# A two-layer diffusion backbone on one core: modulation sums six pieces deep, mixer transfers on one queue, inverses placed by stream step

## The chip, the core and the metric

The kernel runs on one core of one Trainium2 chip. The core has TensorE (PE, matmuls; PEld is its weight loads), VectorE (DVE), ScalarE (ACT), GpSimd (POOL), and SyncE (SP), which only issues transfers. ACT and POOL can issue transfers too. Every engine works through its own instructions in the order in which the program holds them, and waits on semaphores for the others. The metric is the device time of one execution in microseconds (us).

## The reference, cut to what matters

Two layers over 256 latent tokens (and, in the first layer, 256 context tokens), width 2048, all in float32:

```
for l in (0, 1):
    sh1, sc1, g1, sh2, sc2, g2 = split(silu(c) @ ada_w[l] + ada_b[l], 6)     # ada_w[l]: 2048 x 12288
    h = rmsnorm(x) * (1 + sc1) + sh1
    if l == 0:   # even mixer, context hc modulated in the same way from c_ctx
        ka, va, kb, vb, a, b, qa, qb, za = split(h @ ev_w_in)        # 2048 x 7200; context: the first six
        ka, va, qa = silu(conv5(ka, va, qa)); k, q = rope(l2norm(..))
        y_gdn = gated delta rule, chunks of 64, both directions, 8 heads, started from the context's state
                (needs T = inverse of (I + lower part of beta k k^T decay) of every chunk)
        y_na  = neighbourhood attention of 8 heads over grid and context
        y = concat(norm(y_gdn) * silu(za), y_na) @ ev_w_out
    else:        # odd mixer: short gated convolution
        y = (b * conv3(c_ * v)) @ od_w_out
    x = x + g1 * y
    x = x + g2 * (silu(m @ w_gate) * (m @ w_up)) @ w_down            # m = rmsnorm(x) * (1 + sc2) + sh2
out = rmsnorm(x) * final_norm
```

## The kernel before

**Weight streams.** Every large product reads its weights once from HBM. `load_w` fetches 512 KB pieces (`raw`, four buffers in the mixer) on SP's queue; `split_w` makes a rounded half `whi` on ACT and the rest `wlo` on DVE; PE multiplies high by high, low by high and high by low, so that three matmuls stand for one. `fm_stream` makes outputs by feature (weights held, 256 tokens of latent and, where needed, of context streamed), `tm_stream` by token. One step of a stream is one 128-row slice of the contraction.

**Start.** The first layer's sh1 and sc1 come from PE: `start_block(b)` loads 4 MB of `ada_w` in four pieces (`araw0`, four buffers) and multiplies them by the two conditioning vectors (L477); `start_tokens(b)` turns the sums into shift and scale (L488) and modulates two slices of the tokens (transposes of `xn`, then `h_hi`, `h_lo`). The loop runs over b = 0..7, and between two blocks two steps of the first key stream `s0` (512 columns) are put.

**Mixer.** In the order of the code: the second key stream, the gates, `chunk_matrices(1)` (context: Gram matrices, decay, a 31-step substitution on DVE over 32x32 blocks, with a turn through HBM to regroup the blocks: `dl`, `lsol`, `dz`), `inverses` for both head groups (blocks joined to 128x128 on PE, from pieces `xd`, `xdT`, `n32`, `n64` read back from HBM), `chunk_matrices(0)`, the QA and VA streams, the scan over the context, inverses, scores and scan of the latents (`latent_scores`, `latent_quad`), the QB, KB and VB streams (their outputs are staged to HBM through two `nst` buffers, `stage`), attention head by head (`na_scores`, `na_values`; the position bias `br` is read in a strided pattern), the ZA stream, and the output product `ev_w_out`.

**Modulation sums.** The other segments of `ada_w` are summed on DVE: `ada_job` takes one piece `araw` after another (in the mixer 256 KB each, 192 in all, `AB` = 3 buffers), multiplies it by a column of c and adds it to `acc` (L332); PE sums over partitions after 16 pieces (L338). A `Pump` releases R_QB, R_KB, R_ZA or R_WO of them for each step of a stream.

**Order.** The kernel is built with a scheduler that sets each engine's order from its own estimate of durations; the code's order gives priorities. So instructions of stages that lie apart in the code stand mixed in the engines' orders, and `tc.issue_after` only says what an instruction must not be put ahead of. Transfers were issued by SP, and by ACT for stores of results (`kd`, `vd_`, `qTd`, `nd64`, `nd32`, `kb_d`, `vb_d`, `qb_d`, `zd`), half of `lsol` and `dz`, and `br`.

Of the kernel before, what the change touches and what calls it, by code (L numbers as in the profile page):

```python
# [29 lines left out]
D = 2048  # L30
# [12 lines left out]
AB = 3  # L43
R_QB = 1.2
R_KB = 1.8
R_ZA = 1.8
# [59 lines left out]
def body(tc, x, c, ctx, c_ctx, ada_w, ada_b, norm_mix, norm_ffn, ffn_w_gate, ffn_w_up, ffn_w_down,  # L106
# [122 lines left out]

    def split_w(raw, behind=None):  # L230

        hi = wp["pool"].tile([128, 1024], F32R, name="whi", tag="whi", bufs=wp["split"])
        lo = wp["pool"].tile([128, 1024], F32R, name="wlo", tag="wlo", bufs=wp["split"])
        with Stack() as order:
            for ins in behind or ():
                order.enter_context(tc.issue_after(ins.ins))
            acopy(hi, raw)
            DVE.tensor_tensor(lo, raw, hi, op=OP.subtract)  # L238
        return hi, lo

    def w_steps(segs, ks, behind=None):
# [3 lines left out]
        for g in range(0, len(ks), nk):  # L245
            assert ks[g + nk - 1] == ks[g] + nk - 1
            hi, lo = split_w(load_w(segs, ks[g], nk), behind if g // nk in (2, 3) else None)
            for j in range(nk):
                yield ks[g] + j, hi[:, j * W:(j + 1) * W], lo[:, j * W:(j + 1) * W]

# [16 lines left out]
    def tm_stream(segs, ks, lhs, toks, evac, normed=None):  # L267
# [6 lines left out]
        for i, group in grouped(((k, (hi, lo) + lhs(k)) for k, hi, lo in w_steps(segs, ks, normed)), len(ks), head):  # L274
            last = i == len(ks) - 1
            if not last:
                for ti, t in enumerate(toks if group else ()):
                    for g, (hi, lo, lh, ll) in enumerate(group):
# [7 lines left out]
                        for n in range(nb):  # L286
                            PE.matmul(ps[ti][n], b, hi[:, n * 512:(n + 1) * 512], start=False, stop=False)  # L287
# [11 lines left out]
    def fm_stream(segs, ks, ws, evac):  # L299

        ps = [None] * 4
        for i, group in grouped(((k, (k, hi, lo)) for k, hi, lo in w_steps(segs, ks)), len(ks)):
            for f in range(4):
                if i == 0:
                    ps[f] = mmt()
                for g, (k, hi, lo) in enumerate(group):
# [3 lines left out]
                    for j, (wt, mv) in enumerate(((a, h_hi), (a, h_lo), (b, h_hi))):  # L310
                        for n, w in enumerate(ws):
                            if j or i:
                                PE.matmul(ps[f][:, n * 256:(n + 1) * 256], wt, mv(w, k), start=False,  # L313
                                          stop=i == len(ks) - 1 and g == len(group) - 1 and j == 2 and w == ws[-1])
# [5 lines left out]
    def ada_job(pool_, l, seg, kind, gamma=None, width=1024, bufs=2):  # L320

        wr = ada_w[l].rearrange("(k p) n -> p k n", p=128)
        nf = width // 128
        for blk in range(D // width):
            c0 = seg * D + blk * width
            acc = pool_.tile([128, width], F32, name="acc", tag="acc", bufs=1)
            POOL.memset(acc, 0.0)
            SP.dma_start(acc[0:1, :], ada_b[l:l + 1, c0:c0 + width])
            for k in range(KT):
                raw = pool_.tile([128, width], F32, name="araw", tag="araw", bufs=bufs)  # L330
                SP.dma_start(raw, wr[:, k, c0:c0 + width])
                DVE.scalar_tensor_tensor(acc, raw, cT[:, k:k + 1], acc, op0=OP.mult, op1=OP.add)  # L332
                yield
            fs_ = slice(blk * nf, (blk + 1) * nf)
            p = smt()
            if width < 1024:
                for f in range(nf):
                    PE.matmul(p[:, f:f + 1], acc[:, f * 128:(f + 1) * 128], ones[:, 0:1], start=True, stop=True)  # L338
                pc = p
            else:  # L340
                ah = pool_.tile([128, width], F32R, name="ah", tag="ah", bufs=1)
                al = pool_.tile([128, width], F32R, name="al", tag="al", bufs=1)
                split(ah, al, acc, DVE)
                for f in range(nf):
                    for a in (ah, al):
                        PE.matmul(p[0:nf, 0:128], pick[:, nf - 1 - f:2 * nf - 1 - f], a[:, f * 128:(f + 1) * 128],
                                  start=f == 0 and a is ah, stop=f == nf - 1 and a is al)
                g = pool_.tile([16, 128], F32, name="grow", tag="grow", bufs=1)[0:nf]
                acopy(g, p[0:nf, 0:128])
                if kind == "row":  # L350
                    ACT.dma_start(row_d[l, seg][fs_], g)
                    continue
                pc = smt()
                transpose(pc[:, 0:nf], g)
            if kind == "sc":
                DVE.scalar_tensor_tensor(scc[l, seg - 1][:, fs_], pc[:, 0:nf], 1.0, gamma[:, fs_], op0=OP.add, op1=OP.mult)
            else:
                DVE.tensor_copy((shc if kind == "sh" else gcol)[l, seg][:, fs_], pc[:, 0:nf])
        if kind == "row" and width < 1024:
            p = smt()  # L360
            transpose(p[0:16, 0:128], gcol[l, seg])
            g = pool_.tile([16, 128], F32, name="grow", tag="grow", bufs=1)
            DVE.tensor_copy(g, p[0:16, 0:128])
            SP.dma_start(row_d[l, seg], g)
# [39 lines left out]
    def drive(stream, pump=None, n=1):  # L404
        for _ in stream:
            if later:
# [61 lines left out]
    def start_block(b):  # L468

        pr = gdt()  # L470
# [10 lines left out]
    def start_tokens(b, pr):  # L481
        mrow = sp.tile([128, 512], F32, name="mrow", tag="mrow", bufs=2)
        DVE.tensor_copy(mrow, pr)
        p = smt()
# [9 lines left out]
        DVE.tensor_tensor(sc0[:, kk, :], sc0[:, kk, :], g_mix[0][:, kk, None].to_broadcast([128, 2, 2]), op=OP.mult)  # L494
        for k in range(2 * b, 2 * b + 2):
# [3 lines left out]
            for w in range(2):  # L499
# [3 lines left out]
                DVE.tensor_tensor(h_lo(w, k), m, h_hi(w, k), op=OP.subtract)  # L503

# [56 lines left out]
    def head_evac(n, q, c0, done, sums):  # L561
# [3 lines left out]
        def f(i_, p):  # L565
            st_[i_] = kvp.tile([128, 512], F32, name="hst", tag="hst", bufs=4)[:, 0:n * 128]
# [3 lines left out]
            out_t = kvp.tile([128, 4, 4, 128], F32, name="hq", tag="hq", bufs=2)  # L570
# [53 lines left out]
    def ka_evac(q):  # L624
        def done(kt, ss):
            normalise(kt, 4, rstd(kvp, ss, [128, 4, 4], 16, 1.0, "rk"))
            ACT.dma_start(hslice(kd, 0, 4, q), kt.rearrange("p t h e -> p t (h e)"))
        return head_evac(4, q, 0, done, True)

    def va_evac(q):  # L630
        def done(vt, ss):
            ACT.dma_start(hslice(vd_, 0, 4, q), vt.rearrange("p t h e -> p t (h e)"))
        return head_evac(4, q, 8, done, False)

    def qa_evac(q):
        def done(qt, ss):
# [3 lines left out]
            for g in range(2):  # L640
# [6 lines left out]
                ACT.dma_start(qTd[:, q * 4 + g * 2:q * 4 + g * 2 + 2, :], qf)  # L647
# [756 lines left out]
```

## Time and profile before

| what | us |
|---|---|
| median of 3 runs (2838.1, 2841.96, 2846.2) | 2841.96 |
| the profiled execution | 2848.17 |
| its span, first to last instruction | 2846.4 |
| PE busy | 2732.5 |
| DVE busy | 1924.8 |
| ACT busy | 1308.3 |
| mean granted TensorE clock | 0.986 |

The profiled execution is 6.2 us above the median of the others, within what they spread. A busy PE is not PE at its peak: matmuls overlap, and a matmul that is issued late still counts as busy up to its modelled end. So the idle time of a stretch and the granted clock (PEclk, 1.00 is full speed) say more than the share of busy time. In the rows of waits an engine's line and tile come first, then who ended the wait, then the sum, how often, and the longest.

### The profile page before, as it was taken

What the parts mean: (1) busy time and instruction counts of PE and PEld (TensorE: products, weight loads), DVE (VectorE), ACT (ScalarE), POOL (GpSimd) and SP (SyncE); (2) the same over time, 40 slices, a digit from 0 to 9 for tenths busy, and PEclk for the clock granted to TensorE, in tenths of its full rate; (3) what the DMA queues carried; (4) which work ended last, traced back from release to release, by engine and by line L of the source; (5) the groups of instructions that cost most, each with busy time, mean ns of one, the idle gap of its engine ahead of it and who ended that gap; (6) DMA issues with size and microseconds to landing.
All of it is one profiled execution on the core that took longest, in us unless ns stands there. A gap on an engine that the chain in (4) does not pass through costs nothing.

```text
span 2846.4 us, 40363 instructions
## 1 busy us (share of the span) xinstructions
PE 2732.5 (96%) x15113; PEld 2281.6 (80%) x15113; DVE 1924.8 (68%) x2647; ACT 1308.3 (46%) x1945; POOL 51.1 (2%) x77
## 2 busy tenths in 40 slices
PE   5999999989989999999999999999999999999998
PEld 3699989888767778888888878878878888888886
DVE  3387767857667878776677768897678644445665
ACT  3267543222354544444445545444454444444554
POOL 0000001000000000000000000000000000000000
PEclk9999999999999999999999999999999999999999
DMA  9955568777758599987788657998559766656653
GB/s 345 311 177 164 143 208 253 243 225 236 210 170 278 200 318 346 347 285 249 272 305 282 198 175 243 328 319 306 179 179 332 262 188 180 195 186 215 192 192 126
DMA packets 284927, 680.78 MB, mean 239 GB/s; under 512 B 57273, under 2 KB 97313, under 8 KB 283323
## 3 DMA queue, kind: packets, MB, share of 16 engines
q1 hardware_dynamic: 262148, 652.48, 69.4%
q10 hardware_dynamic: 22583, 25.73, 3.0%
q8 instruction: 118, 1.93, 0.3%
q14 instruction: 78, 0.64, 0.1%
HBM read 657.63 MB, written 20.48 MB: 238 GB/s over the span
## 4 chain that ended last, share of the span: by engine, by line
PE 70%; DMA 15%; DVE 9%; issue 3%; ACT 2%; SPq 1%; POOL 0%; ACTq 0%; DVEq 0%; POOLq 0%
PE mm L287 17%; PE mm L285 17%; PE mm L284 17%; DMA araw<-in_ada_w_dram 11%; PE mm L313 7%; DVE acc L332 3%; DVE wlo L238 3%; PE sm L188 2%; PE mm L293 2%; PE mm L295 2%; PE mm L294 2%; DMA raw<-in_od_w_in_dram 1%; DMA acc<-in_ada_b_dram 1%; PE gd L477 1%; ACT whi L169 0%
## 5 line engine op out<-in xcount | busy, mean ns | idle before, releaser
L238 DVE TENSOR_TENSOR wlo<-raw,whi 128x1024 fp32r<-128x1024 f32 x800 | 971.5, 1222 | 452.3 <-ACT whi L169 446.3
L169 ACT ACTIVATE whi<-raw 128x1024 fp32r<-128x1024 f32 x800 | 841.9, 1058 | 875.5 <-PE mm L287 632.4
L332 DVE SCALAR_TENSOR_TENSOR acc<-araw,cT,acc 128x1024 f32<-128x1024 f32 (+1 forms) x416 | 431.2, 1037 | 228.4 <-DMA araw<-in_ada_w_dram 198.8
L285 PE MATMUL mm<-wlo,fhi 128*128 128x512 f32 x1232 | 473.6, 394 | 0.2 <-DVE wlo L238 0.2
L284 PE MATMUL mm<-whi,fhi 128*128 128x512 f32 x1232 | 470.9, 396 | 0.6 <-ACT fhi L1187 0.6
L287 PE MATMUL mm<-whi,flo 128*128 128x512 f32 x1232 | 392.2, 392 | 0.1
L284 PEld LDWEIGHTS mm<-whi,fhi 128*128 128x128 f32 x1232 | 232.4, 189 | 50.4 <-ACT fhi L1187 1.0
L287 PEld LDWEIGHTS mm<-whi,flo 128*128 128x128 f32 x1232 | 231.0, 188 | 50.7 <-DVE flo L1189 0.3
L285 PEld LDWEIGHTS mm<-wlo,fhi 128*128 128x128 f32 x1232 | 232.5, 189 | 48.7 <-DVE wlo L238 0.7
L284 PE MATMUL mm<-whi,ahi 128*128 128x512 f32 x672 | 259.8, 392 | 0.0
L285 PE MATMUL mm<-wlo,ahi 128*128 128x512 f32 x672 | 259.4, 391 | 0.0
L287 PE MATMUL mm<-whi,alo 128*128 128x512 f32 x672 | 209.7, 392 | 0.0
L313 PE MATMUL mm<-hllo,whi 128*128 128x256 f32 x640 | 181.1, 287 | 0.0
L313 PE MATMUL mm<-hlhi,wlo 128*128 128x256 f32 x600 | 169.4, 288 | 2.0 <-issue 1.5
L313 PE MATMUL mm<-hlhi,whi 128*128 128x256 f32 x600 | 167.5, 290 | 1.0 <-DVE hlhi L502 1.0
L172 ACT ACTIVATE ahi<-prodT 128x256 fp32r<-128x256 f32 x176 | 73.0, 417 | 194.7 <-PE mm L285 187.6
L285 PEld LDWEIGHTS mm<-wlo,ahi 128*128 128x128 f32 x672 | 126.2, 188 | 27.5
L284 PEld LDWEIGHTS mm<-whi,ahi 128*128 128x128 f32 x672 | 126.2, 188 | 27.2
L287 PEld LDWEIGHTS mm<-whi,alo 128*128 128x128 f32 x672 | 126.1, 188 | 27.3
L285 PE MATMUL mm<-wlo,dhi 128*128 128x512 f32 x336 | 127.3, 398 | 2.6 <-DVE wlo L238 2.4
L313 PEld LDWEIGHTS mm<-hllo,whi 128*128 128x128 f32 x640 | 124.0, 194 | 0.4
L284 PE MATMUL mm<-whi,dhi 128*128 128x512 f32 x336 | 123.5, 396 | 0.3 <-DVE u_t L1329 0.3
(399 smaller groups left out, 4055.9 us busy)
## 6 DMA issues: line engine op xcount, KB each, us to landing
araw<-in_ada_w_dram SPq DMA_DIRECT2D x288, 512.0 KB
raw<-in_ffn_w_down_dram SPq DMA_DIRECT2D x176, 512.0 KB
raw<-in_ffn_w_gate_dram SPq DMA_DIRECT2D x160, 512.0 KB
raw<-in_ffn_w_up_dram SPq DMA_DIRECT2D x160, 512.0 KB
raw<-in_ev_w_in_dram SPq DMA_DIRECT2D x112, 512.0 KB
araw<-in_ada_w_dram SPq DMA_DIRECT2D x192, 256.0 KB
raw<-in_od_w_in_dram SPq DMA_DIRECT2D x96, 512.0 KB
raw<-in_ev_w_out_dram SPq DMA_DIRECT2D x32, 512.0 KB
```

The source lines that it names most:

```text
L169: ACT.activation(dst, src, AF.Copy)
L172: ACT.activation(hi, src, AF.Copy)
L188: return PE.transpose(dst, src, ident[:n, :n])
L238: DVE.tensor_tensor(lo, raw, hi, op=OP.subtract)
L284: PE.matmul(ps[ti][n], a, hi[:, n * 512:(n + 1) * 512], start=first, stop=False)
L285: PE.matmul(ps[ti][n], a, lo[:, n * 512:(n + 1) * 512], start=False, stop=False)
L287: PE.matmul(ps[ti][n], b, hi[:, n * 512:(n + 1) * 512], start=False, stop=False)
L293: PE.matmul(ps[ti][n], lh(t), hi[:, c_], start=False, stop=False)
L294: PE.matmul(ps[ti][n], lh(t), lo[:, c_], start=False, stop=False)
L295: PE.matmul(ps[ti][n], ll(t), hi[:, c_], start=False, stop=hi is group[-1][0])
L313: PE.matmul(ps[f][:, n * 256:(n + 1) * 256], wt, mv(w, k), start=False, stop=i == len(ks) - 1 and g == len(group) - 1 and j == 2 and w == ...
L332: DVE.scalar_tensor_tensor(acc, raw, cT[:, k:k + 1], acc, op0=OP.mult, op1=OP.add)
```

## The change

- **Sums.** `ada_job` keeps only its 1024-wide form; the mixer's sums become `ada_mixer`: six pieces are loaded ahead (`AHEAD` = `AB` = 6), `acc` has two buffers, each sum is ordered behind the last `wlo` (`issue_after(last_lo)`), and the closing matmuls come three sums late (`LAG`). R_QB goes from 1.2 to 0.6, R_ZA from 1.8 to 1.5.
- **Queue.** All the mixer transfers that ACT issued are issued by SP.
- **Inverses.** The read-back is split off (`load_offdiag`, `load_diag`) and stands ahead of the QB stream; the inverses run from `plan` at counted stream steps 30, 32, 79 and 80, and their first matmuls are ordered behind the stream's last (`last_mm`). `chunk_matrices(0)` and the context's scan move behind step 32, scores and scan of the latents behind step 80.
- **Half of the second key group early.** A stream `s1` over 256 of its 512 columns runs in turn with `s0` in the start, from block 1 on; it uses the two `gd` PSUM banks, and the start's sums move to the `sm` banks. The other 256 columns follow as a stream of their own, in which deferred work is released at every second step.
- **Buffers.** `hst` has six buffers instead of four; the heads' outputs share the two `xdT` buffers.

```diff
-R_QB = 1.2
+P_INV = (30, 32, 79, 80)
+AHEAD = 6
+LAG = 3
+R_QB = 0.6
-AB = 3
+AB = 6
-R_ZA = 1.8
+R_ZA = 1.5
...
+    def ada_mixer(pool_, parts):
...
+            raws[i] = pool_.tile([128, 512], F32, name="araw", tag="araw", bufs=AB)
+            SP.dma_start(raws[i], wr[:, k, c0:c0 + 512])
+
+        def total(i):
+            n, k = divmod(i, KT)
+            with tc.issue_after(last_lo[0]):
+                DVE.scalar_tensor_tensor(accs[n], raws.pop(i), cT[:, k:k + 1], accs[n], op0=OP.mult, op1=OP.add)
...
+        for i in range(AHEAD):
+            load(i)
+        N = len(blocks) * KT
+        for i in range(N + LAG):
+            if i < N:
+                total(i)
+                load(i + AHEAD)
+            if i >= KT + LAG - 1 and (i - LAG + 1) % KT == 0:
+                close((i - LAG + 1) // KT - 1)
+            yield
...
+    def drive(stream, pump=None, n=1, every=1, counts=False):
+        for i, _ in enumerate(stream):
+            steps[0] += counts
+            while counts and plan and plan[0][0] <= steps[0]:
+                plan.pop(0)[1]()
+            if later and i % every == every - 1:
...
-        pr = gdt()
+        pr = smt()
...
-    s0 = fm_stream([(wv, C_KA, 512)], ks, [0, 1], ka_evac(0))
+    s0 = fm_stream([(wv, C_KA, 512)], ks, [0, 1], ka[0])
+    s1 = fm_stream([(wv, C_KA + 512, 256)], ks, [0, 1], ka[1], gdt)
...
+    both = in_turn(s0, s1)
     for b in range(8):
-        start_tokens(b, sums)
+        start_tokens(b, sums, both if b else iter(()))
         if b < 7:
-            next(s0), next(s0)
             sums = start_block(b + 1)
...
-    drive(fm_stream([(wv, C_KA + 512, 512)], ks, [0, 1], ka_evac(1)))
+    drive(fm_stream([(wv, C_KA + 768, 256)], ks, [0, 1], lambda f, p: ka[1](f + 2, p)), every=2)
...
-        ACT.dma_start(nd64, n64)
-        ACT.dma_start(nd32, n32)
+        SP.dma_start(nd64, n64)
+        SP.dma_start(nd32, n32)
...
-                (SP, ACT)[d].dma_start(lsol[p0:p0 + 16], dl[b, :, d * 16:(d + 1) * 16, :].rearrange("r n c -> n r c"))
+                SP.dma_start(lsol[p0:p0 + 16], dl[b, :, d * 16:(d + 1) * 16, :].rearrange("r n c -> n r c"))
...
     parts = chunk_matrices(1)
-    xdTs = [inverses(parts, q) for q in range(2)]
-    parts = chunk_matrices(0)
...
+    def second_inverse():
+        nonlocal parts, off, diag
+        xdTs.append(inverses(off, diag[1], 1))
+        parts = chunk_matrices(0)
+        for q in range(2):
+            scan(q, 1, xdTs[q])
+        xdTs.clear()
+        off = load_offdiag(parts)
+        diag = [load_diag(parts[2], q) for q in range(2)]
+
+    def latents():
+        xdTs.append(inverses(off, diag[1], 1))
+        ATs = [latent_scores(q) for q in range(2)]
+        o_ts.extend(latent_quad(q, xdTs[q], ATs[q]) for q in range(2))
...
+    plan += [(P_INV[0], first_inverse), (P_INV[1], second_inverse), (P_INV[2], first_inverse), (P_INV[3], latents)]
...
-            ACT.dma_start(br[half * 64:half * 64 + 64], src)
+            SP.dma_start(br[half * 64:half * 64 + 64], src)
```

How the built orders differ at three places follows. L188, L284, L285, L287, L313, L332, L338, L477, L488, L918, L927, L938 and L960 of before are L191, L291, L292, L294, L321, L389, L396, L533, L546, L1000, L1009, L1020 and L1042 now.

PE, in the last block of the start, before: sums of `ada_w` (`gd<-araw`), shift and scale (`mrow`), token transposes (`xn`), then stream `s0`.

```order
L477 MATMUL gd<-araw_1016,cT_120 32x512 x4
L477 MATMUL gd<-araw_1023,cT_120 32x512 x4
L477 MATMUL gd<-araw_1030,cT_120 32x512 x4
L488 MATMUL sm<-cs,mrow 128x2 x4
L188 MATMUL sm<-cs,xn 128x128 x8
L313 MATMUL mm<-hlhi,whi 128x256 x4
```

The same place now (`mm` is `s0`, `gd` is `s1`):

```order
L321 MATMUL mm<-hclo,whi 128x256
L321 MATMUL mm<-hlhi,wlo 128x256
L321 MATMUL mm<-hchi,wlo 128x256
L321 MATMUL gd<-hlhi,whi 128x256
L321 MATMUL gd<-hchi,whi 128x256
L321 MATMUL gd<-hllo,whi 128x256
L533 MATMUL sm<-araw_1138,cT_120 32x512 x4
L321 MATMUL gd<-hclo,whi 128x256
L321 MATMUL gd<-hlhi,wlo 128x256
L321 MATMUL gd<-hchi,wlo 128x256
```

Matmuls of both key streams now stand between the sums. Ahead of the last L488 there were 332 of the streams' matmuls, and ahead of the last L546 there are 479; on SP 12 `raw` pieces stood ahead of the last piece of the start's `ada_w`, and now 14.

SP, where the latents' inverse pieces are read back around the end of the first VB stream, before (the last two of eight such reads `xd`, `xdT` from `dz`; `kT`, `vtok` for the context's scan; `araw` for the sums; `raw` a stream's weights):

```order
L864 DMA xd<-dz 32x16x32
L864 DMA xdT<-dz 32x16x32
L781 DMA kT<-kTd 128x1024
L776 DMA vtok<-vd__139 128x2x512
L331 DMA araw<-in_ada_w_dram 128x512 x3
L226 DMA raw<-in_ev_w_in_dram 128x2x512
```

The same read-back now, in the second KB stream:

```order
L915 DMA dz<-zsol 8x8x1024 x2
L915 DMA dz<-lsol 8x8x1024 x2
L384 DMA araw<-in_ada_w_dram 128x512 x5
L936 DMA xdT<-dz 32x16x32
L936 DMA xd<-dz 32x16x32 x2
```

Before, three pieces of the sums stood behind the eight reads and the two loads for the scan; now five stand ahead of the reads.

PE, at the end of the mixer, before: the latents' scan (`state`, `R`, `vn`) among attention (`kb`, `PT`) and the end of the ZA stream, then `ev_w_out` (`yhi`).

```order
L293 MATMUL mm<-whi,hlhi 128x512
L294 MATMUL mm<-wlo,hlhi 128x512
L295 MATMUL mm<-whi,hllo 128x512
L927 MATMUL gd<-state,qT 128x128 x4
L938 MATMUL gd<-R,xdT 128x128 x4
L1112 MATMUL sm<-PT,vb 128x256 x4
L1088 MATMUL sm<-kb,qb 128x512
L1089 MATMUL sm<-bq,cs 128x256
L960 MATMUL gd<-vn,AT 128x128 x4
```

The same end now:

```order
L1020 MATMUL gd<-R,xdT 128x128 x4
L1042 MATMUL gd<-vn,AT 128x128 x4
L1000 MATMUL gd<-state,kT 128x128 x4
L1009 MATMUL gd<-state,qT 128x128 x4
L1020 MATMUL gd<-R,xdT 128x128 x4
L1042 MATMUL gd<-vn,AT 128x128 x4
L1187 MATMUL gd<-kb,qb 128x512
L1188 MATMUL gd<-bq,cs 128x256
```

The last three steps of the scan (L1000 to L1042 each) now stand behind all the stream matmuls that don't need their result.

And SP, at the first attention heads, now (`br` was on ACT's queue; each pair of `br` has one buffer and waits for DVE to have read the pair before):

```order
L1180 DMA br<-in_ev_rpb_dram 64x6x64 x2
L1202 DMA vb<-vb_d 128x4x128
L384 DMA araw<-in_ada_w_dram 128x512
L229 DMA raw<-in_ev_w_in_dram 128x1024 x2
L384 DMA araw<-in_ada_w_dram 128x512
L1180 DMA br<-in_ev_rpb_dram 64x6x64 x2
L229 DMA raw<-in_ev_w_in_dram 128x1024
L384 DMA araw<-in_ada_w_dram 128x512
```

Weights of the ZA stream now stand behind pairs of `br`.

More of the change, by code (lines that the diff above doesn't have):

```diff
@@ L332, in ada_job @@
                 DVE.scalar_tensor_tensor(acc, raw, cT[:, k:k + 1], acc, op0=OP.mult, op1=OP.add)
                 yield
-            fs_ = slice(blk * nf, (blk + 1) * nf)
+            fs_ = slice(blk * 8, (blk + 1) * 8)
             p = smt()
[L336 to L359, printed above, removed]
-            p = smt()
[L361 to L364, printed above, removed]
+            ah = pool_.tile([128, 1024], F32R, name="ah", tag="ah", bufs=1)
@@ new lines, in ada_job @@
+            al = pool_.tile([128, 1024], F32R, name="al", tag="al", bufs=1)
+            split(ah, al, acc, DVE)
+            for f in range(8):
+                for a in (ah, al):
+                    PE.matmul(p[0:8, 0:128], pick[:, 7 - f:15 - f], a[:, f * 128:(f + 1) * 128],
+                              start=f == 0 and a is ah, stop=f == 7 and a is al)
+            g = pool_.tile([16, 128], F32, name="grow", tag="grow", bufs=1)[0:8]
+            acopy(g, p[0:8, 0:128])
+            if kind == "row":
+                ACT.dma_start(row_d[l, seg][fs_], g)
+                continue
@@ L402, in flush @@
             f(*args)
-    def drive(stream, pump=None, n=1):
-        for _ in stream:
-            if later:
+    plan = []
+    steps = [0]
+    def drive(stream, pump=None, n=1, every=1, counts=False):
[4 more added lines that the diff above has]
+            if later and i % every == every - 1:
                 f, args = later.pop(0)
@@ L864, in inverses @@
                 SP.dma_start(m_, dz[v, b, q].rearrange("d t (r c) -> r (d t) c", r=32))
+        return xd, xdT
+    def inverses(off, diag, q):
+        n64, n32 = (t[:, q * 8:q * 8 + 8, :] for t in off)
+        xd, xdT = diag
         for w, nn in ((32, n32), (64, n64)):
```

157 lines of the change are left out of this document (103 added, 54 removed).

## The prediction

> **What bounds the kernel now.** I read the page's head first, then the busy times by stretch, then who waits for whom in the stretches that the change touches.
>
> ```profile
> PE 2732.5 (96%) x15113; PEld 2281.6 (80%) x15113; DVE 1924.8 (68%) x2647; ACT 1308.3 (46%) x1945; POOL 51.1 (2%) x77
> ...
> core 0: us, PE busy (x) PEld busy (x) DVE busy (x) ACT busy (x) POOL busy (x), PEclk, DMA share, GB/s
> 0.00:140.00 140.00, 105.08 (x728) 65.93 (x729) 45.98 (x118) 38.95 (x57) 4.74 (x8) 0.98 1.00 331
> 140.00:350.00 210.00, 205.28 (x1710) 202.97 (x1709) 165.30 (x346) 139.83 (x312) 8.85 (x18) 1.00 0.53 158
> 350.00:500.00 150.00, 139.89 (x1556) 135.89 (x1555) 105.63 (x186) 63.58 (x109) 13.76 (x23) 0.98 0.76 234
> 500.00:600.00 100.00, 87.85 (x727) 77.03 (x727) 70.03 (x151) 23.88 (x48) 7.12 (x7) 0.93 0.79 245
> 600.00:700.00 100.00, 98.72 (x892) 89.99 (x891) 71.91 (x108) 28.34 (x49) 1.58 (x3) 1.00 0.72 227
> 700.00:860.00 160.00, 144.05 (x725) 114.76 (x724) 99.04 (x206) 75.46 (x170) 0.53 (x1) 0.96 0.63 190
> 860.00:960.00 100.00, 94.27 (x414) 75.61 (x414) 78.25 (x118) 45.30 (x69) 1.49 (x2) 0.97 0.73 246
> 960.00:2846.40 1886.40, 1857.31 (x8375) 1519.40 (x8373) 1288.66 (x1421) 893.00 (x1135) 13.00 (x15) 0.99 0.73 246
> ```
>
> The reader is to see three regimes. Up to 140 us the DMA engines are full (share 1.00) and PE waits for them. From 140 on PE is the bound: what can be won is its idle time (stretch less PE busy) and what a lowered clock costs (stretch times 1 less PEclk). That is 4.7 us in 140:350; 10.1 + 12.2 + 1.3 = 23.6 idle and 3 + 7 = 10 of clock in 350:700; 16 and 6.4 in 700:860; 5.7 and 3 in 860:960. Behind 960 nothing is moved, so 1886 us stay as they are.
>
> **Start.** The 479 - 332 = 147 more matmuls of the key streams that PE now does before the start's last sums come out of what it does behind them, at the bound's pace:
>
> ```profile
> 149.07 12.59 PE mm L313 x105
> ...
> PE gd L477 <- DMA araw<-in_ada_w_dram: 22.0, 10, 9.5
> ```
>
> 12.59 / 105 = 0.12 us each, so 147 take 17.6 us off. There is room: 35 us of the first 140 are idle, and a matmul L477 whose sums wait also counts as busy. The price is DMA: two `raw` pieces of 512 KB more ahead of the last `ada_w` piece, 1.05 MB at the 331 GB/s of the first stretch, 3.2 us. The start's sums now alternate with token tiles in the two `sm` banks, so a block's first sum waits for one token tile of the block before; four `araw0` buffers hold 4 MB, 12 us of transfers, which covers it. Net -14.4 us. If the extra matmuls held the `araw0` buffers up too, I would lose 4 us of it; if the loads hid, win 3.
>
> **Sums and inverses, 350 to 700 us.** In this order: PE's waits, DVE's, ACT's, and the worst moment.
>
> ```profile
> PE mm L309 <- DVE nst L166: 5.1, 1, 5.1
> PE gd L887 <- ACT Y L169: 3.8, 1, 3.8
> PE gd L880 <- issue: 3.4, 2, 3.1
> PE gd L769 <- DVE gm L765: 2.6, 3, 1.4
> PE gd L801 <- DVE kT L166: 2.3, 1, 2.3
> PE sm L338 <- DVE acc L332: 2.0, 1, 2.0
> ...
> DVE acc L332 <- DMA araw<-in_ada_w_dram: 49.9, 37, 5.5
> DVE acc L332 <- DMA acc<-in_ada_b_dram: 11.5, 4, 4.6
> ...
> ACT whi L169 <- DMA lsol<-dl: 12.9, 1, 12.9
> ACT vd L942 <- DVE nst L166: 10.6, 1, 10.6
> ACT Y L169 <- DMA araw<-in_ada_w_dram: 7.3, 1, 7.3
> ...
> 570.54 0.75 DVE L332 SCALAR_TENSOR_TENSOR acc<-araw,cT,acc 128x512 f32<-128x512 f32 x1 [5.50 <-DMA araw<-in_ada_w_dram]
> 574.73 0.68 DVE L166 COPY nst<-mm 128x512 f32<-128x512 f32 x1
> 575.47 0.79 PE L309 MATMUL mm<-h,whi 128*128 128x512 f32 x1 [5.10 <-DVE nst L166]
> 586.15 0.95 PE L887 MATMUL gd<-xdT,Y 32*32 32x32 f32 x53 [3.84 <-ACT Y L169]
> ```
>
> DVE sits 61 us before sums whose piece has not landed, with copies and splits queued behind. At 565 to 575 the piece stands on SP behind eight reads of the inverse, DVE waits 5.5 us, the copy that frees a PSUM bank comes late, and PE stands 5.1 us; then ACT, which issues a store, waits and PE stands 3.8 more. Waits of this kind are 5.1 + 3.8 + 2.6 + 2.3 + 2.0 = 15.8 us of PE. With six pieces loaded ahead and the sum behind the split they should go. L880 (3.4) waits for the read-back, which now has the whole QB stream to land. With these 19.2 of 23.6 idle us goes the same share of the 10 us of clock: 27.3.
>
> What is late next: DVE has as many sums as before and the substitution among them; the inverses' halves follow each other on PE with little between; and SP now waits for what ACT waited for. Sixty-eight transfers move to SP (counted from the code: 24 staged outputs, 16 `br`, 8 `lsol`, 20 others); the dearest kind takes 0.62 us to issue, so SP spends at most 42 us more in some 800, out of time in which it now waits for buffers (152.7):
>
> ```profile
> L1081 ACTq DMA_DIRECT2D br<-in_ev_rpb_dram x16: 602/617/704, 712.4 to 802.7; - x16
> ...
> SPq L226 <- DVE wlo L238: 152.7, 83, 7.6
> ...
> 803.20 0.39 PE L293 MATMUL mm<-whi,hlhi 128*128 128x512 f32 x1
> 803.43 0.40 PE L294 MATMUL mm<-wlo,hlhi 128*128 128x512 f32 x1
> ```
>
> A blocked SP is covered by the four `raw` pieces ahead: a 512-wide matmul follows the one before by 0.23 us, a piece of VB feeds 24 of them, so four last 22 us, against 12.9 for ACT's longest wait on a transfer. I cost the moved stores at nothing here; were that cover used up, each such wait would cost its length. On POOL the clearing of `acc` now stands behind that of `xdT`, which waits for the scan; the second `acc` gives it 16 sums of time. The heads' outputs share the two `xdT` buffers and wait for their store, a whole stream later (384 matmuls, 46 us); six `hst` only loosen. For new stalls I give a quarter of the 27 back, between nothing (all of 33.6 won) and all of it. Taken: -20 us.
>
> **Attention and the scan's end, 700 to 860 us.**
>
> ```profile
> PE mm L284 <- ACT whi L169: 3.8, 2, 3.5
> PE sm L1089 <- DVE bq L1084: 3.4, 1, 3.4
> ...
> ACT whi L169 <- DMA br<-in_ev_rpb_dram: 8.5, 1, 8.5
> ...
> 725.37 12.92 DMA br<-in_ev_rpb_dram
> ...
> 808.46 1.16 PE L938 MATMUL gd<-R,xdT 128*128 128x128 f32 x8 [0.59 <-DVE R L921]
> 814.32 1.13 PE L960 MATMUL gd<-vn,AT 128*128 128x128 f32 x8 [1.68 <-DVE o_t L932]
> ```
>
> ACT stood 8.5 us with a `br` transfer ahead of a weight half, and PE 3.8; that goes with its 1.7 us of clock (3.4 us at half speed): -5.5. Against it the scan's last three steps now have no stream matmuls between them. Where such a step was bare, PE waited 0.59 + 1.68 = 2.3 us; three make 6.8, and about 1.2 of clock: +8. Both ends: 0, if attention fills it, and 16, if each step also pays for a lowered clock. Net +2.5.
>
> **Sum.** -14.4 - 20 + 2.5 = -32 us. The profiled execution, 2848, is 6 above the median 2842; the sum is a difference, so it goes on the median: 2810.
>
> **Rivals.**
> - *More is won.* All visible loss of 350:700 goes (33.6) and half of the 22.4 in 700:860, with the start: -59, 2783. For it: nearly every long wait there names a transfer. Against: other waits move up.
> - *Only the start counts.* What the sums free is eaten by DVE (70% busy in 500:600) or later waits: -14.4, 2828.
> - *Six are not six.* On SP, `raw`, stores and read-backs stand between the pieces; a piece behind a blocked transfer is as late as one of three. Half of the 20 is lost: 2820.
> - *Stores behind loads.* In SP's one queue a store can stand behind six pieces and four `raw`, 3.6 MB, 14.8 us at the 245 GB/s of 500:600. If the staged values (`vb_d`) and the gates (`zd`) are read back bare, each costs about 10 us: +20, 2830. Against: the DMA share there is 0.63 to 0.79, so the queue is seldom that full. The Trainium skill ("DMA: Bandwidth & Descriptors", on queues, rings and completion order) says that each DMA engine serves the queues that have work in turns, so that a store on ACT's own queue gets its turn beside SP's loads; by that rule this case is the likelier, and the trace of before, with ACT's stores on their own queue, can't show it.
> - *Slower: SP is closed by `br`.* A pair of `br` waits for the pair before to land and be read, 12.9 us by the row above, and the ZA weights stand behind it. A piece that comes late also needs its own transfer and split,
>
> ```profile
> 900.29 4.86 DMA raw<-in_ev_w_out_dram
> ...
> 726.43 1.06 ACT L169 ACTIVATE whi<-raw 128x1024 fp32r<-128x1024 f32 x1 [4.00 <-DMA araw<-in_ada_w_dram]
> 720.64 1.22 DVE L238 TENSOR_TENSOR wlo<-raw,whi 128x1024 fp32r<-128x1024 f32 x1
> ```
>
> 12.9 + 4.9 + 2.3 = 20 us, against four pieces of 12 matmuls at 0.23, 11 us: 9 lost for each of seven heads, +63, 2873. From 32 / 7 = 4.6 us a head on it decides. Against: PE has attention and scan to do meanwhile, and only one of eight `br` was waited for by PE (3.4).
>
> **How the numbers follow.** The forecast has 0.47, more is won 0.13, only the start 0.13, six not six 0.07, stores behind loads 0.08, slower 0.12. A measurement can tell about 0.3% from no change, 8.5 us. Below 2833.4 lie the forecast with nearly all of its chance, the richer case, and most of the three poorer ones: 0.79 faster. Above 2850.5 lies the `br` case: 0.12. The rest, 0.09, is the same. The range takes in the richer case with 7 us for a better start and reaches up past 2830 to a mild form of the `br` case: 2776 to 2846; the forecast alone has 2792 to 2826.
>
> **What would show it.** In the new profile the first 140 us should hold some 147 more stream matmuls, and the last L533 land by about 138 us. DVE's wait for `araw` should fall from 49.9 to under 15 between 350 and 700, PEclk there rise to 0.98 or more, and ACT's waits for `lsol`, `br` and `dz` vanish. The scan's end should show PE waits for `R` and `vn` of about 7 us. I am wrong if SP's waits for DVE or PE at L1180 or L1142 turn into waits of PE for `whi`, or if DVE still stands before sums.

## The result, and the profile after

The changed kernel takes 2822.8 us (median of 6 runs, 2819.7 to 2824.7) against 2843.3 for the kernel before: ratio 0.9929, 95% interval 0.9916 to 0.9943, some 20 us less. One of the six runs of the kernel before took 6233 us and is not in the ratio. Forecast were 2810, a range of 2776 to 2846, and 2792 to 2826 for the likeliest case alone. The profiled execution has a span of 2822.0 us.

First the busy times by stretch, with the columns of the table shown for before (stages that end earlier are cut earlier, at 840 and 940 us):

```profile
0.00:140.00 140.00, 110.05 (x803) 74.72 (x803) 45.80 (x110) 38.68 (x55) 1.74 (x7) 1.00 1.01 333
140.00:350.00 210.00, 202.14 (x1676) 198.68 (x1669) 156.62 (x339) 137.42 (x314) 13.14 (x20) 0.99 0.49 149
350.00:500.00 150.00, 139.69 (x1541) 136.53 (x1540) 111.25 (x187) 60.41 (x96) 10.12 (x18) 0.95 0.78 245
500.00:600.00 100.00, 99.79 (x683) 92.18 (x683) 79.73 (x170) 29.37 (x58) 9.26 (x12) 1.00 0.81 256
600.00:700.00 100.00, 89.77 (x925) 74.96 (x923) 60.05 (x85) 26.75 (x39) 1.05 (x2) 0.96 0.76 242
700.00:840.00 140.00, 127.87 (x694) 104.95 (x694) 99.41 (x218) 71.72 (x178) 0.21 (x1) 0.95 0.62 197
840.00:940.00 100.00, 95.64 (x430) 77.53 (x428) 79.18 (x122) 44.55 (x67) 0.84 (x2) 0.97 0.73 247
940.00:2822.00 1882.00, 1854.83 (x8382) 1517.99 (x8381) 1288.03 (x1420) 893.00 (x1137) 13.94 (x16) 0.99 0.73 247
```

The start is fuller (110.05 us busy, before 105.08), 500:600 has no idle time left (99.79, before 87.85), and everything behind the mixer takes 1882 us against 1886. But 350:500 has fallen to a clock of 0.95 (0.98 before), and 600:700 has lost 10 us where before it lost 1.3. A hole was closed and others opened. Who waits there, from the view of waits in 350 to 700 us, with two rows of 700 to 840 us behind:

```profile
DVE acc L389 <- DMA araw<-in_ada_w_dram: 24.5, 13, 4.9
ACT nst L167 <- DMA kb_d<-nst: 11.5, 1, 11.5
ACT nst L1141 <- DMA qb_d<-nst: 8.9, 3, 7.9
PE mm L317 <- ACT nst L1141: 5.3, 2, 3.9
PE gd L962 <- DVE xd L977: 5.2, 2, 4.1
PE gd L975 <- issue: 4.9, 2, 3.0
...
PE gd L1042 <- ACT vn L1038: 1.0, 2, 0.5
...
PE gd L1020 <- DVE R L1003: 0.2, 1, 0.2
```

The sums' wait fell from 49.9 + 11.5 us to 24.5, and no wait for `lsol`, `dz` or `br` is left among ACT's. In their place ACT waits for the staging buffers `nst`, and PE waits behind it and inside the inverse (L962, L975). DVE's wait for `br` stays (11.9 us before and 14.6 after, in 350 to 860 us). The six longest PE waits shown of before add up to 19.2 us; the three above are 15.4 of it again, under other names.

The new wait at QB's end is worth reading in order of time. Before, and then after:

```profile
392.99 0.61 ACTq L632 DMA_DIRECT2D vd__139<-hq  x1
...
402.19 0.32 ACTq L1051 DMA_DIRECT2D qb_d<-nst  x1
...
406.61 0.38 ACT L1050 ACTIVATE nst<-mm 128x256 f32<-128x256 f32 x1 [1.65 <-DMA qb_d<-nst]
```

```profile
387.75 0.53 SPq L692 DMA_DIRECT2D vd__139<-hq  x1
388.37 1.34 SPq L1142 DMA_DIRECT2D qb_d<-nst  x2
...
396.13 0.70 ACT L1141 ACTIVATE nst<-mm 128x256 f32<-128x256 f32 x2 [7.85 <-DMA qb_d<-nst]
396.56 0.58 PE L317 MATMUL mm<-h,whi 128*128 128x256 f32 x1 [3.94 <-ACT nst L1141]
```

The last heads' store `vd` (1 MB) used to be issued 9 us ahead of the first staged stores. Now QB's first group ends earlier and they follow it by 0.6 us: the two staging buffers come free 7.85 us late, and PE stands 3.94 us. The clock falls with it:

```profile
390.00:400.00 10.00, 6.06 (x38) 5.86 (x38) 3.18 (x5) 0.70 (x2) 2.06 (x2) 0.79 0.92 328
400.00:410.00 10.00, 10.00 (x75) 10.00 (x75) 7.03 (x8) 4.13 (x4) 0.70 (x1) 0.87 0.79 202
```

0.79 and 0.87 are 6.83 us at half clock (4.13 and 2.70 us of it in the two slices), so the 3.94 us cost 3.4 more. The Trainium skill ("TensorE: Matmul & The Clock Gate", on the clock gate) says that the clock halves after an idle window of some 3.4 us and that windows run freely; this trace agrees: by its clock records the half-clock pieces are 3.41 or 6.83 us long (the last, at the trace's end, 11.5), and the pieces at full clock between them are whole multiples of 3.41 us.

### The profile page after: what moved, and what is told of

Read it like the earlier page. It is cut to its first block, busy times and chain, and to the rows that moved or that the text cites. A ratio compares the mean times of both kernels' runs of the same rounds, so it can differ in the third digit from the quotient of the medians.

```text
span 2822.0 us, 40405 instructions
## 1 busy us (share of the span) xinstructions
PE 2719.8 (96%) x15113; PEld 2277.5 (81%) x15113; DVE 1920.1 (68%) x2647; ACT 1301.9 (46%) x1943; POOL 50.3 (2%) x77
## 4 chain that ended last, share of the span: by engine, by line
PE 78%; DMA 10%; DVE 6%; ACT 3%; issue 2%; SPq 1%; DVEq 0%; POOL 0%; ACTq 0%
PE mm L294 19%; PE mm L291 19%; PE mm L292 19%; PE mm L321 7%; DMA araw<-in_ada_w_dram 5%; PE mm L300 2%; PE mm L301 2%; PE mm L302 2%; DVE wlo L243 2%; PE sm L191 2%; DMA raw<-in_od_w_in_dram 1%; PE sm L533 1%; DVE acc L346 1%; DVE acc L389 1%; PE gd L321 1%
## 5 line engine op out<-in xcount | busy, mean ns | idle before, releaser
L292 PE MATMUL mm<-wlo,fhi 128*128 128x512 f32 x1232 | 472.4, 392 | 0.0
L291 PE MATMUL mm<-whi,fhi 128*128 128x512 f32 x1232 | 470.7, 396 | 0.0
L294 PE MATMUL mm<-whi,flo 128*128 128x512 f32 x1232 | 392.2, 392 | 0.1
L346 DVE SCALAR_TENSOR_TENSOR acc<-araw,cT,acc 128x1024 f32<-128x1024 f32 x224 | 287.3, 1283 | 130.2 <-DMA araw<-in_ada_w_dram 123.5
L294 PEld LDWEIGHTS mm<-whi,flo 128*128 128x128 f32 x1232 | 230.8, 188 | 51.1 <-DVE flo L1288 0.5
L292 PEld LDWEIGHTS mm<-wlo,fhi 128*128 128x128 f32 x1232 | 231.8, 188 | 48.7
L291 PEld LDWEIGHTS mm<-whi,fhi 128*128 128x128 f32 x1232 | 231.9, 188 | 48.2
L291 PE MATMUL mm<-whi,ahi 128*128 128x512 f32 x672 | 259.8, 392 | 0.0
L292 PE MATMUL mm<-wlo,ahi 128*128 128x512 f32 x672 | 259.3, 391 | 0.0
L294 PE MATMUL mm<-whi,alo 128*128 128x512 f32 x672 | 209.8, 392 | 0.0
L321 PE MATMUL mm<-hllo,whi 128*128 128x256 f32 x608 | 172.9, 289 | 0.0
L321 PE MATMUL mm<-hlhi,whi 128*128 128x256 f32 x570 | 161.7, 292 | 2.2 <-DVE hlhi L561 1.9
L389 DVE SCALAR_TENSOR_TENSOR acc<-araw,cT,acc 128x512 f32<-128x512 f32 x192 | 142.7, 747 | 29.1 <-DMA araw<-in_ada_w_dram 27.3
L321 PE MATMUL mm<-hlhi,wlo 128*128 128x256 f32 x570 | 157.8, 289 | 0.0
L292 PEld LDWEIGHTS mm<-wlo,ahi 128*128 128x128 f32 x672 | 126.2, 188 | 27.7
L294 PEld LDWEIGHTS mm<-whi,alo 128*128 128x128 f32 x672 | 126.1, 188 | 27.3
L291 PEld LDWEIGHTS mm<-whi,ahi 128*128 128x128 f32 x672 | 126.2, 188 | 27.1
L292 PE MATMUL mm<-wlo,dhi 128*128 128x512 f32 x336 | 126.4, 396 | 2.2 <-DVE wlo L243 2.2
L291 PE MATMUL mm<-whi,dhi 128*128 128x512 f32 x336 | 123.8, 397 | 0.6 <-DVE u_t L1428 0.6
```

What stands on the lines that cost most here:

```text
L291: PE.matmul(ps[ti][n], a, hi[:, n * 512:(n + 1) * 512], start=first, stop=False)
L292: PE.matmul(ps[ti][n], a, lo[:, n * 512:(n + 1) * 512], start=False, stop=False)
L294: last_mm[0] = PE.matmul(ps[ti][n], b, hi[:, n * 512:(n + 1) * 512], start=False, stop=False).ins
L321: last_mm[0] = PE.matmul(ps[f][:, n * 256:(n + 1) * 256], wt, mv(w, k), start=False, stop=i == len(ks) - 1 and g == len(group) - 1 and j = ...
L389: DVE.scalar_tensor_tensor(accs[n], raws.pop(i), cT[:, k:k + 1], accs[n], op0=OP.mult, op1=OP.add)
```

## The experiments

All times are medians; "before" was run beside each. The ratio is to before, with its 95% interval; 0.001 is 2.8 us.

| run | what it is | us | ratio |
|---|---|---|---|
| (the change) | | 2822.8 | 0.9929 [0.9916, 0.9943] |
| no_early | changed, without the early half | 2830.1 | 0.9961 [0.9945, 0.9977] |
| three_deep | changed, 3 pieces in flight | 2846.3 | 1.0016 [1.0001, 1.0031] |
| no_pace | changed, sums not behind the split | 2830.9 | 0.9947 [0.9935, 0.9960] |
| all_act | changed, transfers back on ACT | 2821.4 | 0.9930 [0.9911, 0.9950] |
| inverses_early | changed, inverses at steps 1, 2, 60, 62 | 2823.5 | 0.9922 [0.9909, 0.9934] |
| stores_apart | changed, staged stores alone on ACT | 2820.5 | 0.9930 [0.9912, 0.9948] |
| stage3 | changed, 3 staging buffers | 2815.2 | 0.9909 [0.9889, 0.9930] |
| readback_act_3 | stage3, read-backs on ACT | 2825.6 | 0.9926 [0.9913, 0.9940] |
| before_six | before, 6 `araw` buffers | 2825.9 | 0.9932 [0.9919, 0.9945] |
| start_alone | before, early half | 2856.4 | 1.0045 [1.0033, 1.0057] |
| six_and_start | before, both | 2838.8 | 0.9984 [0.9974, 0.9995] |
| six_start_stage3 | before, both and 3 staging buffers | 2826.3 | 0.9942 [0.9930, 0.9955] |

**The depth of the sums: three_deep, before_six, no_pace.** Theory: most of the gain is that DVE no longer stands before sums whose piece has not landed.

```diff
-AB = 6
-AHEAD = 6
+AB = 3
+AHEAD = 3
```

> Three pieces of the sums in flight instead of six; pacing, queue and inverses as in the changed kernel. By the prediction's middle term (-20) nearly all of it hangs on depth: DVE's waits for araw between 350 and 700 us go back from 24.5 towards 50 us and the time rises by 12 to 20, 2835 to 2843. Rival, six are not six (a blocked SP makes any piece late): at most +5, 2823 to 2828. Rival, three are better, since SP is held up less: 2815 to 2820.

It is +0.0087 on the changed kernel, 25 us: the whole gain and a little more. The waits of 350 to 700 us, and PE's longest:

```profile
DVE acc L389 <- DMA araw<-in_ada_w_dram: 73.3, 45, 6.0
...
617.13 1.87 PE L396 MATMUL sm<-cs,acc 128*128 128x1 f32 x8 [5.37 <-DVE acc L389]
```

DVE is back to waiting (73.3 us, 45 times), and PE stands behind a sum. "Six are not six" and "only the start counts" fall here. The other side, in the kernel before:

```diff
-AB = 3
+AB = 6
```

> The kernel before with six araw buffers instead of three and nothing else of the change: its sums are issued where they were, unpaced. Three pieces in flight cost the changed kernel 24 us (three_deep 2846 against 2823). Theory depth: most of it comes from buffers alone, also here: 2820 to 2828, and no part but depth and start is needed. Theory pacing: buffers help only where loads are issued six ahead and the sum stands behind a split; here at most -5: 2837 to 2842.

One number gives 0.9932, which is the change's 0.9929 within their intervals. DVE's wait in the same stretch:

```profile
DVE acc L332 <- DMA araw<-in_ada_w_dram: 13.0, 8, 5.0
```

49.9 us became 13.0 without any pacing, and the wait for `acc` 8.0 instead of 11.5: theory depth holds, and "buffers help only where loads are issued six ahead" was wrong. Whether the pacing adds something to depth:

```diff
-            with tc.issue_after(last_lo[0]):
-                DVE.scalar_tensor_tensor(accs[n], ...)
+            DVE.scalar_tensor_tensor(accs[n], ...)
```

> Six pieces ahead, but a sum may be issued as soon as the order allows, not behind the last weight split (the issue_after of the sums is dropped); all else as in the changed kernel. Theory pacing: sums run ahead of the splits, DVE's waits for araw grow from 24.5 us past 45 and the time rises by 8 to 20: 2831 to 2843. Theory depth: six ahead are enough, 2819 to 2827.

+0.0018, 5 us, with intervals that overlap: between the two expectations. DVE's wait for `araw` rose only to 29.1 us, not past 45. Among what grew in 350 to 700 us are ACT's wait for `qb_d` (8.9 to 13.5 us) and PE's waits for `xd` (5.2 to 8.1), for ACT's `s` (L1194, 4.3, a new row) and for `qb` (3.6, new); PE's wait for `nst` at L317 fell from 5.3 to 1.9.

**The early half: no_early, start_alone, six_and_start.** The changed kernel, with the streams taken in turn cut to the first:

```diff
-    both = in_turn(s0, s1)
+    both = in_turn(s0, None)     # None: a step without matmuls
```

> The second key stream's first half (256 columns) is streamed whole behind the start instead of between the start's sums; all else as in the changed kernel (2822.8). If the prediction's start term is right, PE does some 147 fewer matmuls before the start ends and does them later at 0.12 us each: +10 (what the first 150 us of the two traces show as won) to +14.4 (the term), 2833 to 2837. Rival, only the start counts: the whole gain goes, 2843. Rival, the DMA bound of the start hides it either way: 2823.

```profile
0.00:140.00 140.00, 103.62 (x712) 64.25 (x716) 41.42 (x107) 35.83 (x52) 1.74 (x7) 0.98 0.98 326
```

The first stretch loses 6.4 us of work again, and the run is +0.0032, 9 us. So inside the changed kernel the early half is worth some 9 us. In the kernel before (its `start_block`, `start_tokens` and the key streams as in the change's diff, `hst` left at four):

```diff
+    s1 = fm_stream([(wv, C_KA + 512, 256)], ks, [0, 1], ka[1], gdt)
+    both = in_turn(s0, s1)
...
-    drive(fm_stream([(wv, C_KA + 512, 512)], ks, [0, 1], ka_evac(1)))
+    drive(s1)
+    drive(fm_stream([(wv, C_KA + 768, 256)], ks, [0, 1], lambda f, p: ka[1](f + 2, p)), every=2)
```

> The kernel before with the start of the change alone: half of the second key group is streamed beside the start's sums (the block's sums in the sm banks, the early half's result in the gd banks), three araw buffers, transfers and inverses as before. Taking the early half out of the changed kernel cost 7 us (2830 against 2823). If the start adds up with the rest: 2832 to 2836 where before is 2842. Prediction's term: 2827. Rival, it only pays once the sums no longer block DVE behind it: 2838 to 2844.

> The kernel before with six araw buffers and the early half of the second key group, and nothing else of the change: no pacing, transfers on ScalarE as before, inverses where they were. Six buffers alone give 0.9932 of before, the start some 0.997. Theory (two small edits are the change, the rest of it costs what it gains): 2814 to 2820, below the changed kernel. Rival, the parts overlap (the start's gain is eaten by a wait further on): 2821 to 2827.

Both theories missed: the same edit costs 13 us alone (1.0045), and 15 on top of six buffers (0.9984 against 0.9932). The start itself is as good as in the changed kernel: the 900th stream matmul (L313 and L309, then L321 and L317 and their like) begins at 219.5 us before, 208.9 after, 208.2 in start_alone. What is lost comes later. QB's end in six_and_start:

```profile
389.96 0.52 ACTq L637 DMA_DIRECT2D vd__139<-hq  x1
391.99 1.20 ACTq L861 DMA_DIRECT2D dz<-lsol  x1
396.34 0.66 ACT L1065 ACTIVATE nst<-mm 128x256 f32<-128x256 f32 x2 [2.06 <-DMA vd__139<-hq]
396.78 0.58 PE L310 MATMUL mm<-h,whi 128*128 128x256 f32 x1 [5.28 <-ACT nst L1065]
...
406.75 0.38 ACT L1065 ACTIVATE nst<-mm 128x256 f32<-128x256 f32 x1 [9.75 <-DMA qb_d<-nst]
```

PE stands twice here, 5.28 us and then 3.96, and its clock is 0.71 in 390:400 and 0.84 in 400:410. In the kernel before, PE has no idle time in these 20 us and a clock of 1.00. The first wait is one that the changed kernel doesn't have. In the kernel before, the pool of `nst` is opened where that of the heads' outputs (`hq`) was closed, and by the row of 396.34 the first copy into `nst` waits for the 1 MB store that reads `hq`. In start_alone this wait of ACT is 4.86 us and PE's behind it 6.30. The change puts `hq` into `xdT`'s buffers, in another pool, and there the first copy is made at 387.62 us, ahead of the store's issue. The second wait is for the staged stores, as in the changed kernel, but behind other transfers: `vd` had landed before they were issued (396.75), and the two `dz` stores of 256 KB ahead of them on ACT's queue move their packets from 395.5 to 403.9 us. The first store of `dz` is issued at 365 us before and at 369 in before_six, well ahead of QB's end; with the early start it is issued at 382 and 391, and meets it. In the changed kernel the early half doesn't make the staging wait: no_early has it too (ACT 8.74 us, PE 3.32), with the stores again 0.66 us behind `vd`. That these stalls are all that start_alone and six_and_start lose isn't shown.

**The staging buffers: stage3, six_start_stage3.**

```diff
-NST = 2
+NST = 3
```

> Three staging buffers instead of two between the streams' results and their stores on SyncE; all else as in the changed kernel. In the trace after, ACT waits 8.9 + 11.5 us for stores that stand on SP, and PE 1.6 + 4.1 us behind the first, with 6.8 us at half clock. If these waits cost what they show, -6 to -9: 2814 to 2817. Rival, the wait moves to the next late thing (the piece for the sum, the inverse's read-back): 2820 to 2825.

> As six_and_start, with three staging buffers instead of two. Stores stand on ScalarE's queue here and not behind SyncE's loads, and with six buffers alone ScalarE waited 5.0 + 4.4 us for them. Theory (the 7.6 us that a third buffer won in the changed kernel was made by its stores on SyncE): 0 to -3 against six_and_start. Rival (two buffers are too few on any queue): -5 to -8, 2808 to 2813.

In the kernel before with both edits the third buffer takes 12 us back (0.9984 to 0.9942, intervals apart): two are too few with the stores on ACT's queue as well, and the theory that SyncE made them scarce falls. In the changed kernel it gives -0.0020, 6 us: the six runs lie at 2811.1 to 2819.3, all below the change's 2819.7 to 2824.7, though the intervals of the two ratios overlap. It is the fastest version run. How it wins is only half shown. At QB's end ACT still waits, but PE waits 0.45 us behind it instead of 3.94, and the clock there stays at 1.00 and 0.98 (0.79 and 0.87 with two buffers). PE waits for `whi` instead, at 409 us and at 428:

```profile
393.47 0.38 ACT L1141 ACTIVATE nst<-mm 128x256 f32<-128x256 f32 x1 [6.25 <-DMA qb_d<-nst]
...
PE mm L317 <- ACT whi L172: 5.0, 1, 5.0
...
PE mm L321 <- ACT whi L172: 3.5, 1, 3.5
```

With two and with three buffers (six_and_start and six_start_stage3), the 4000th matmul of the trace begins at 503.0 and 502.3 us, the 4500th at 588.6 and 582.6, the 7000th at 1014.5 and 1002.0: there the third buffer pays later, in the KB and VB streams and in the attention, where the same two buffers carry bigger stores.

**The queue: all_act, stores_apart, readback_act_3.** All moved transfers back on ACT:

```diff
-            SP.dma_start(dst(i), st_)
+            ACT.dma_start(dst(i), st_)
```

and the same for `br`, `zd`, the heads' stores, `nd64`, `nd32`, and one of each pair of `lsol` and `dz`.

> All the moved transfers (staged stores, br, gates, the inverse's writes, the heads' stores) go back from SyncE to ScalarE's queue as in the kernel before; all else as in the changed kernel. By the prediction ACT's waits for br (8.5 us before) and lsol (12.9) come back and PE loses 5 to 10 us: 2828 to 2833. Rival, stores behind loads: ACT's waits for staged buffers (8.9 + 11.5 us in the trace after) and PE's 5.7 us with them vanish, with their lowered clock 9 us less: 2814. Rival, the queue doesn't matter: 2823.

0.9930: nothing, as the third theory said. ACT's wait for `br` doesn't come back with the queue, and that for `lsol` only with 5.7 us.

```profile
386.06 0.52 ACTq L692 DMA_DIRECT2D vd__139<-hq  x1
386.68 1.49 ACTq L1142 DMA_DIRECT2D qb_d<-nst  x2
...
396.19 0.38 ACT L1141 ACTIVATE nst<-mm 128x256 f32<-128x256 f32 x1 [9.61 <-DMA qb_d<-nst]
```

The wait for the staging buffer is 9.61 us here and 7.85 on SyncE. Then the staged stores alone on ACT, apart from `vd`:

> Only the staged stores (qb_d, kb_d, vb_d) go to ScalarE's queue, apart from the heads' 1 MB store vd, which stays on SyncE; two staging buffers, all else as in the changed kernel. In the trace after, vd is issued at 387.75 and the first qb_d store at 388.37 on the same queue; ACT then waits 7.85 us for a staging buffer. With both on ScalarE's queue (all_act) it waited 9.61. Theory own queue: the small store no longer stands behind the 1 MB one, the wait falls under 4 us and the time by some 4 to 8: 2815 to 2819. Rival, the transfer engines are full (share 0.92 at 390 to 400 us), whatever the queue: the wait stays at 7 to 10 us, 2820 to 2826.

```profile
385.65 0.53 SPq L692 DMA_DIRECT2D vd__139<-hq  x1
...
385.93 1.00 ACTq L1142 DMA_DIRECT2D qb_d<-nst  x2
...
392.43 0.38 ACT L1141 ACTIVATE nst<-mm 128x256 f32<-128x256 f32 x1 [6.26 <-DMA qb_d<-nst]
394.02 1.80 POOL L931 MEMSET xdT<- 128x2048 f32 x1 [49.25 <-DMA vd__139<-hq]
```

The small store, issued 0.28 us behind the big one on another queue, lands 1.6 us ahead of it (392.4 against 394.0). By the Trainium skill ("DMA: Bandwidth & Descriptors", on queues, rings and completion order) a transfer engine serves the queues in turns; the overtaking agrees with that, but a turn is worth 1.6 us of 7.85 here. PE's wait falls from 3.94 to 2.34 us and the clock of 390:410 stays at 1.00, but the runs tell no time from it (0.9930; the profiled execution, 2814.9, is the fastest of five with a median of 2820.5). The wait is between the two theories. Last, with three staging buffers, the inverse's read-backs on ACT:

```diff
-        SP.dma_start(n64, parts[0])
+        ACT.dma_start(n64, parts[0])
```

and so for `n32`, `xd` and `xdT`.

> Three staging buffers as in stage3 (2815.2), and the read-backs of the inverse (n64, n32, xd, xdT) issued by ScalarE instead of SyncE. Theory (the sums' pieces stand on SyncE behind read-backs that wait for their writes, DVE waits 4.9 us, PE 4.3): 3 to 6 less than stage3, 2809 to 2812. Rival, ScalarE is held by the read-backs instead and weight halves come late, as before the change with lsol (12.9 us): 2819 to 2828.

```profile
ACT whi L172 <- DMA xd<-dz: 19.7, 1, 19.7
...
PE mm L321 <- ACT whi L172: 12.7, 1, 12.7
```

The rival was right: ACT stands 19.7 us with the read-backs, and PE 12.7; of the third buffer's gain nothing can be seen (0.9926), though the interval overlaps that of stage3 (0.9909). So by the trace it matters which engine issues a transfer that has to wait for data that are not there yet; for the 68 moved ones the runs show no difference.

**The inverses' place: inverses_early.**

```diff
-P_INV = (30, 32, 79, 80)
+P_INV = (1, 2, 60, 62)
```

> The inverses are queued behind stream steps 1, 2, 60 and 62 instead of 30, 32, 79 and 80, so that the scheduler places them where their read-back lands; all else as in the changed kernel. Theory (the counted steps set the inverses late and bare, which eats 10 us or so of the middle term): the scan ends earlier and PE's stalls by L962 and L975 (3.2 + 1.2 + 2.1 + 4.3 us, with 6.8 us of lost clock) shrink: 2808 to 2817. Rival, the read-backs aren't there earlier and PE waits longer: 2826 to 2840. Rival, the place doesn't matter: 2820 to 2825.

```profile
600.00:700.00 100.00, 98.12 (x864) 86.27 (x864) 63.35 (x93) 30.12 (x49) 1.58 (x3) 1.00 0.69 221
700.00:840.00 140.00, 124.75 (x651) 100.85 (x650) 98.16 (x210) 67.83 (x164) 0.41 (x1) 0.94 0.64 204
```

0.9922 against 0.9929: the third expectation, or a gain too small to see. In the busy times PE has 98.12 us in 600:700, where after has 89.77, but 124.75 instead of 127.87 in 700:840 at a clock of 0.94, and ahead of it 137.53 instead of 139.69 in 350:500 and 96.83 instead of 99.79 in 500:600. The 8.4 us of idle time that went from 600:700 came back, 5.1 ahead of it and 3.1 behind. The length of a wait is not its price.

## Why the prediction was right, point by point

The case it called likeliest came in, 13 us above its centre. The sum was -32; measured are -20.

- *Start, -14.4.* no_early gives 9. The step that was too large is the 147 matmuls, which were counted from the order; in time they are fewer. The start's own sums, by the view of one tile in before and after (first and last start at the colon's right), end at 142.7 us and not at the 138 forecast:

```profile
L477 PE MATMUL gd<-araw,cT x88: 592/592/617, 99.7 to 134.8; 128*32 128x512 f32 x88
```

```profile
L533 PE MATMUL sm<-araw,cT x96: 592/592/617, 106.8 to 142.7; 128*32 128x512 f32 x96
...
DVE mrow L540 <- PE sm L533: 48.5, 7, 11.2
...
PE sm L533 <- DMA araw<-in_ada_w_dram: 8.3, 4, 3.3
```

By 142.7 us PE has done 453 stream matmuls, where the kernel before had done 362 by that time: 91 x 0.12 = 10.9 us. The 479th begins at 146.4 instead of 157.1, 10.7 earlier. PE waits 8.3 us for `araw` (22.0 before), but DVE waits 48.5 us for a block's sums (15.0 before), which PE now does between stream steps. The early half is not the reason for that: it is 46.9 us in no_early.

- *Sums, -20.* The cause is right and the size too: 25 by three_deep, 19 by before_six. The wait fell to 24.5 us, not under 15, and the clock of 350:500 fell to 0.95 instead of rising to 0.98. The step that failed is "a quarter given back for new stalls" (7 us): the PE waits shown above are 15.4 us, and three pieces of 6.83 us between 350 and 699 ran at half clock, 10 us lost, as much as before. By the prediction's own account (idle time, and stretch times 1 less PEclk), 350:700 lost 33.6 us before and loses 32.3 now, but only 14.5 in before_six, which reaches the end of the mixer at the same time, 940 us:

```profile
0.00:140.00 140.00, 103.64 (x705) 65.04 (x705) 44.12 (x109) 37.00 (x53) 1.56 (x6) 0.96 0.98 326
140.00:350.00 210.00, 204.38 (x1697) 201.58 (x1698) 164.74 (x345) 140.46 (x314) 11.98 (x21) 1.00 0.54 160
350.00:500.00 150.00, 145.22 (x1619) 141.69 (x1618) 115.37 (x208) 66.51 (x112) 15.50 (x24) 0.99 0.80 253
500.00:600.00 100.00, 95.80 (x984) 85.40 (x984) 76.38 (x155) 27.65 (x54) 6.60 (x6) 0.97 0.85 269
600.00:700.00 100.00, 99.03 (x684) 89.30 (x683) 70.00 (x108) 28.68 (x52) 1.58 (x3) 1.00 0.71 230
700.00:840.00 140.00, 122.18 (x619) 98.71 (x620) 84.36 (x184) 71.35 (x158) 0.00 (x0) 0.95 0.60 178
840.00:940.00 100.00, 95.06 (x432) 77.08 (x431) 80.06 (x121) 45.83 (x69) 1.05 (x2) 0.98 0.72 247
```

Six buffers alone won their 19 us where the prediction looked for them. The rest of the change, set against these rows in the same way, wins 12 us in the start and 5 behind 700, and loses 4 in 140:350 and 18 in 350:700. That is 5 lost on balance by this account, which doesn't see a stall that counts as busy, and nothing by the end of the mixer. three_deep is 0.0016 above before, though it has the early half: with three pieces, too, the rest of the change gains nothing on balance.

- *Moved transfers, 0, and ACT's wait for `br`, -5.5.* The price was right. For the gain no run speaks: ACT's waits for `lsol` and `br` are gone, but all_act, with the transfers back on ACT, has none for `br` and 5.7 us for `lsol` and is no slower; and before_six, where ACT still waits 10.8 us for `lsol`, is as fast as the change. What the 8.5 us for `br` cost in the kernel before stays open.
- *Bare scan steps, +8.* They cost 1.0 + 0.2 us of waits for `vn` and `R`, not 7: attention fills them, the lower end that was named.
- *Rivals.* "Stores behind loads" had the right stores and the wrong reason: they wait at QB's end, behind another store, and on either queue. "SP closed by `br`" did not show: PE's only wait for `whi` in 700 to 840 us is one of 3.0.
- *The sum itself.* It added the terms as if each stood alone. On the kernel before six buffers give -19, the start +13, and both -4.5 us. In the changed kernel the early half pays all the same (9). The traces name one reason, the heads' outputs in `xdT`'s buffers: without them the first copy into `nst` waits for the 1 MB store, and PE stands 5.3 and 6.3 us. Pacing (5 us, intervals overlapping) may be another; all_act and inverses_early say that the queue and the counted steps are not. How much each is worth stays open: the heads' outputs in `xdT`'s buffers, the scan's place behind the second inverse and the six `hst` buffers were not tried alone.

## What to carry to other kernels

Try the one-number part of a large change first: six buffers instead of three gave here what a rewrite of the order, the queues and the start gave together. Before a stage is moved forward, look at which large transfers will be under way when it ends, whether its output buffers last as long as one of them takes (8 us here), and whether their memory is still being read by one. Terms of a sum that change when other work ends aren't additive; where two of them meet in one buffer, one should be costed with the other in place.

## What was not expected of the hardware

Two 128 KB stores issued 0.3 to 0.7 us behind a 1 MB store held their buffers so long that ACT waited 5.9 to 9.6 us for them, on the same queue as it (5.94 in no_pace and 7.85 in the change on SyncE's, 9.61 on ACT's) and on another (6.26); issued 9 us behind it, ACT waited 1.65. In six_and_start, where the 1 MB store had landed, two 256 KB stores of `dz` ahead of them on ACT's queue went with a wait of 9.75.
